# Pair weights requested before the last norm's squares, and a third block-product pair in the last MLP quarter

## The chip, the cores and the metric

One core of a Trainium2 chip runs the whole kernel. The metric is the device time of one execution in microseconds (us), the median of several runs. The engines are PE (TensorE, matrix products), ACT (ScalarE), DVE (VectorE), POOL (GpSimd) and SP (SyncE, which here issues DMAs). Each engine works through its own queue strictly in the order in which the program was built, and waits at an instruction until the results that it needs are there.

## The reference, cut to what matters

A decoder block on 512 tokens of 1024 channels: two attention mixers, then an MLP, then a last norm. The change touches the MLP's second product and the last norm alone:

```python
h = modulate(rmsnorm(x, g_mlp[layer]), sh_m, sc_m)
x = x + gt_m[:, None, :] * (jnp.square(jax.nn.relu(h @ w_fc1[layer])) @ w_fc2[layer])
...
return rmsnorm(x, g_final)
```

`w_fc1` is 1024 x 4096, `w_fc2` 4096 x 1024, everything float32.

## The kernel before, in words

Activations are kept transposed: a tile is 128 channels by 512 tokens, and `x` is eight such tiles (`xt`). A float32 operand is split into a high part (rounded to the PE's format by ACT) and a low part (the remainder, by DVE), and each product is three matmuls: high x high, high x low, low x high (`mm3`, L196).

The MLP runs in four quarters (`for qq in range(4)`). A quarter makes eight hidden tiles with `w_fc1` (24 matmuls of 512 columns each, `dense`), squares and splits them (`unit_relu` L913, `unit_parts` L918), and multiplies them with a quarter of `w_fc2`, adding the result to `xt`. The hidden tiles are made in the order `UNITS`; the first two of the next quarter are made ahead (`held`).

The second product goes by pairs of output tiles (`fc2_pair` L891). A pair is a 2 x 2 block matrix: two output tiles by two halves of the 1024 hidden channels of the quarter, times two halves of hidden channels by two halves of the tokens. With seven products of blocks in place of eight (sums of blocks taken beforehand) it needs 7 x 12 = 84 matmuls of 256 columns where plain products need 96. `pair_weights` (L826) prepares a pair: two DMAs of 512 KB (`raw[1]`, `raw[0]`), four sums of 128 x 512 on POOL (s1, s3, s2, s4 in that order: s2 is made from s1, s4 from s2), and the high and low parts of all blocks on ACT (L823) and DVE (L824). `pair_tiles` (L868) runs the products on PE in the order a11, s1, s3, s2, a12, s4, a22. Two accumulators are used twice: a12 adds into the bank of a11, and a22 into that of s3, so ACT first copies the bank out (L876 `u` after a11, L880 `e` after s3), and DVE adds s1's bank into `e` (L881) and s2's into `u` (L884) before s4 and the next pair use those banks. `sink` then adds the blocks into `xt` (DVE L898 to L905, and one sum `v` on POOL, L900).

In the last quarter only the first four output tiles go as pairs (`NH2 = 4` of the eight stay plain). I call those pairs A (tiles 0 and 1) and B (tiles 2 and 3). Tiles 4 to 7 are plain products by token halves: for each half 4 x 24 matmuls of 256 columns (L197 to L199), `mlp_out` (L808) with its square, then the norm of that half (`Stats.rstd` L149) and eight products into output tiles (L1018). So the first half's norm and output run under the second half's products. `Stats.add` (L128) takes a tile's square on ACT (L130) and adds it on DVE (L144); L911 and L813 scale the tile for the output on ACT.

What sets the order: nothing is ordered by hand here. The scheduler of the framework places instructions engine by engine when the program is built, by priority (the order of the code, with `tc.high_priority()` blocks first) and by its own estimate of what is ready. Buffers come from rotating pools: four for raw weights, three each for `w_hi` and `w_lo`, five of tag `p` (a pair's sums' high and low parts take four), three of tag `pT` (the four sums of a pair go through them), five of tag `tmp`. A buffer is written again only when its last reader is done.

Of the kernel before, what the change touches and what calls it, by code (L numbers as in the profile page):

```python
# [16 lines left out]
P = 128  # L17
S = 512
# [18 lines left out]
NH1 = 4  # L37
NH2 = 4
NPRE = 4
# [7 lines left out]
def block_kernel(ctx: ExitStack, tc: tile.TileContext, d):  # L47
# [777 lines left out]

    def pair_weights(src0, src1):  # L826

# [6 lines left out]
        for x_, y_ in ((a21, a22), (a11, a21), (0, a11), (2, a12)):  # L834
            t = sb.tile([P, S], F32, name="wsum", tag="pT", bufs=NB["pT"])
            nc.gpsimd.tensor_tensor(t, sums[x_] if isinstance(x_, int) else x_, y_, op=ALU.add)  # L836
            sums.append(t)
# [52 lines left out]

    def fc2_pair(qq, n):  # L891
        w = pair_weights(d["w_fc2"][qq, n], d["w_fc2"][qq, n + 1])

        def sink(pa, pb, pc, u, e):
            g0 = modb[:, GTM + n:GTM + n + 1]
            g1 = ngt[:, n + 1:n + 2]
            x0, x1 = xt[n], xt[n + 1]
            nc.vector.scalar_tensor_tensor(x0[:, T0], pa, g0, x0[:, T0], op0=ALU.mult, op1=ALU.add)  # L898
            v = tmp("v2")
            nc.gpsimd.tensor_tensor(v[:, T1], u, e, op=ALU.add)  # L900
            v1 = tmp("v1")[:, 0:HS]
            nc.vector.tensor_tensor(v1, u, pb, op=ALU.add)
            nc.vector.scalar_tensor_tensor(x0[:, T1], v1, g0, x0[:, T1], op0=ALU.mult, op1=ALU.add)
            nc.vector.tensor_tensor(v[:, T0], u, pc, op=ALU.add)
            nc.vector.scalar_tensor_tensor(x1, v, g1, x1, op0=ALU.mult, op1=ALU.add)  # L905

        pair_tiles(w, ub, sink)
        if qq == 3:
            for j in (n, n + 1):
                st2.add(xt[j])  # L910
                nc.scalar.activation(xt[j], xt[j], AF.Copy, scale=cols[:, C_GFIN + j:C_GFIN + j + 1])  # L911

    def unit_relu(pa, r):  # L913
# [48 lines left out]
    for qq in range(4):  # L962
# [11 lines left out]
        for i, n in enumerate(UNITS):  # L974
# [5 lines left out]
            else:  # L980
                w = wsplit(d["w_fc1"][8 * qq + n], (KT, P))
                pa = psum(("acc", "acc", "m", "o")[i % 4])
                dense(pa, w, h2)
            unit_parts(n, unit_relu(pa, tmp("relu")), ub, keep, qq == 3)

        held = {}
        if qq < 3:
            for i in range(2):
# [4 lines left out]
                held[i] = unit_relu(pa, r)  # L993
        nf = KT - NH2 if qq == 3 else KT
        for n in range(0, nf, 2):
            fc2_pair(qq, n)

    for k in range(4):
# [5 lines left out]
        ub.setdefault("12", []).append((hi, lo))  # L1004
    ws = [wsplit(d["w_fc2"][3, n], (KT, P), n < KT - 2) for n in range(nf, KT)]
    for hf, tok in enumerate(HALVES):
# [128 lines left out]
```

## Time and profile before

| | us |
|---|---|
| median of 3 runs | 817.91 |
| lowest and highest | 816.78 and 817.96 |
| the profiled execution's own time | 819.28 |
| its span in the profile | 817.5 |
| outside the span | 1.8 |

The profile is of one execution, which took 1.4 us longer than the median. Times below are us from the start of its span. The last quarter's second product starts at 759.31. A page line counts an engine as busy while any of its instructions runs. PE's instructions overlap, so a wait of PE shows as a jump between the starts of two neighbours: in the unstalled stretches they start about 0.12 us apart for 256 columns. A bracket behind a row gives the idle time before that instruction and what ended it.

### The profile page before, as it was taken

How to read it: one execution, taken by the hardware profiler on the slowest of the kernel's cores; microseconds unless marked ns; L12 is line 12 of the kernel's file. 1: busy time of each engine (PE TensorE's matmuls, PEld its weight loads, DVE VectorE, ACT ScalarE, POOL GpSimd, SP SyncE). 2: the span in 40 equal slices, each digit the busy share in tenths (PEclk: the TensorE clock that was granted, in tenths of full speed). 3: DMA queues.
4: the chain of work that ended last, by engine and by line, in shares of the span. 5: the costliest groups of instructions: out<-in, count | busy, mean ns of one | idle time of the engine just before them, and what ended most of it. 6: DMA issues, size and time to landing. Idle time of an engine off the chain costs nothing.

```text
span 817.5 us, 11881 instructions
## 1 busy us (share of the span) xinstructions
PE 795.0 (97%) x4444; PEld 645.4 (79%) x4444; DVE 605.3 (74%) x1186; ACT 385.7 (47%) x734; POOL 127.1 (16%) x116
## 2 busy tenths in 40 slices
PE   6999999999999999999999999999999999999896
PEld 3887668665577666888888998898899988998895
DVE  6989569878667778767676748886768676877854
ACT  4358437465324443323333446644564456445741
POOL 1000000001000000002200004450435043614200
PEclk9999999999999999999999999999999999999998
DMA  9972341010052034884357302333233422332303
GB/s 353 309 235 101 135 150 53 26 52 26 26 181 77 1 103 145 289 308 159 104 170 242 104 25 79 111 105 121 78 104 98 135 78 83 100 128 83 100 1 103
DMA packets 31004, 99.76 MB, mean 122 GB/s; under 512 B 3521, under 2 KB 5761, under 8 KB 30946
## 3 DMA queue, kind: packets, MB, share of 16 engines
q1 hardware_dynamic: 30880, 98.89, 36.3%
q8 instruction: 35, 0.57, 0.3%
q14 instruction: 23, 0.19, 0.1%
q0 software_dynamic: 64, 0.11, 0.0%
q10 hardware_dynamic: 2, 0.00, 0.0%
HBM read 96.89 MB, written 2.10 MB: 121 GB/s over the span
## 4 chain that ended last, share of the span: by engine, by line
PE 81%; DVE 5%; DMA 5%; ACT 4%; issue 3%; POOL 2%; SPq 0%; DVEq 0%; POOLq 0%; ACTq 0%
PE ps_acc L197 10%; PE ps_acc L199 10%; PE ps_acc L198 10%; PE ps_s L865 8%; PE ps_t L865 7%; PE ps_t L382 4%; PE ps_o L563 4%; DMA w_raw<-in_w_fc_dram 3%; PE ps_s L197 2%; PE ps_s L198 2%; PE ps_s L199 2%; PE ps_s L635 2%; PE ps_o L648 2%; POOL wsum L836 1%; PE ps_acc L258 1%
## 5 line engine op out<-in xcount | busy, mean ns | idle before, releaser
L183 ACT ACTIVATE w_hi<-w_raw 128x1024 fp32r<-128x1024 f32 x76 | 80.3, 1059 | 129.0 <-PE ps_acc L198 47.9
L184 DVE TENSOR_TENSOR w_lo<-w_raw,w_hi 128x1024 fp32r<-128x1024 f32 x76 | 99.4, 1309 | 51.4 <-ACT w_hi L183 51.1
L337 ACT ACTIVATE p<-p,nm 128x128 f32<-128x128 f32 (+3 forms) x96 | 53.3, 556 | 59.4 <-DVE nm L335 58.0
L199 PE MATMUL ps_acc<-hh,w_lo 128*128 128x512 f32 x200 | 80.2, 401 | 0.0
L198 PE MATMUL ps_acc<-hl,w_hi 128*128 128x512 f32 x200 | 79.7, 399 | 0.0
L197 PE MATMUL ps_acc<-hh,w_hi 128*128 128x512 f32 x200 | 79.6, 398 | 0.0
L370 DVE COPY pT<-ps_t 128x512 f32<-128x512 f32 (+1 forms) x72 | 42.3, 598 | 29.2 <-PE ps_o L563 16.4
L823 ACT ACTIVATE ws_hi<-wsum 128x512 fp32r<-128x512 f32 x56 | 35.3, 631 | 58.0 <-POOL wsum L836 55.4
L107 DVE SCALAR_TENSOR_TENSOR junk<-w_raw,cb 128x1024 bf16<-128x1024 f32 x32 | 38.5, 1220 | 19.0 <-DMA w_raw<-in_w_ada_dram 19.0
L836 POOL TENSOR_TENSOR wsum<-wsum,w_raw 128x512 f32<-128x512 f32 x28 | 45.6, 1630 | 25.8 <-DVE ws_lo L824 25.5
L836 POOL TENSOR_TENSOR wsum<-w_raw 128x512 f32<-128x512 f32 x28 | 39.2, 1400 | 65.2 <-DMA w_raw<-in_w_fc_dram 57.0
L824 DVE TENSOR_TENSOR ws_lo<-wsum,ws_hi 128x512 fp32r<-128x512 f32 x56 | 42.9, 797 | 4.9 <-PE ps_t L865 2.1
L198 PEld LDWEIGHTS ps_acc<-hl,w_hi 128*128 128x128 f32 x200 | 37.6, 188 | 10.9 <-issue 4.2
L197 PEld LDWEIGHTS ps_acc<-hh,w_hi 128*128 128x128 f32 x200 | 37.6, 188 | 10.8 <-issue 3.9
L199 PEld LDWEIGHTS ps_acc<-hh,w_lo 128*128 128x128 f32 x200 | 37.6, 188 | 10.4 <-issue 3.8
L197 PE MATMUL ps_acc<-h2h,w_hi 128*128 128x512 f32 x112 | 43.6, 389 | 0.0
L198 PE MATMUL ps_acc<-h2l,w_hi 128*128 128x512 f32 x112 | 43.6, 389 | 0.0
L199 PE MATMUL ps_acc<-h2h,w_lo 128*128 128x512 f32 x112 | 43.6, 389 | 0.0
L865 PE MATMUL ps_t<-t,ws_hi 128*128 128x256 f32 x224 | 40.5, 281 | 0.7 <-DVE t L953 0.4
L382 PEld LDWEIGHTS ps_t<-ident,p 128*128 128x128 f32 x240 | 27.6, 141 | 16.1 <-issue 5.4
L824 DVE TENSOR_TENSOR w_lo<-w_raw,w_hi 128x1024 fp32r<-128x1024 f32 (+1 forms) x28 | 31.1, 1110 | 10.2 <-ACT w_hi L823 10.2
L382 PE MATMUL ps_t<-ident,p 128*128 128x128 f32 x240 | 37.1, 279 | 0.0
(522 smaller groups left out, 2250.2 us busy)
## 6 DMA issues: line engine op xcount, KB each, us to landing
w_raw<-in_w_fc_dram SPq DMA_DIRECT2D x64, 512.0 KB, 3.3
w_raw<-in_w_ada_dram SPq DMA_DIRECT2D x32, 512.0 KB, 4.3
w_raw<-in_w_z_dram SPq DMA_DIRECT2D x25, 512.0 KB, 4.1
w_ada<-in_w_ada_dram SPq DMA_DIRECT2D x16, 512.0 KB, 5.7
w_raw<-in_w_c_dram SPq DMA_DIRECT2D x8, 512.0 KB, 4.8
w_raw<-in_w_o_dram SPq DMA_DIRECT2D x8, 512.0 KB, 4.8
w_raw<-in_w_out_dram SPq DMA_DIRECT2D x8, 512.0 KB, 3.3
w_raw<-in_w_g_dram SPq DMA_DIRECT2D x8, 448.0 KB, 6.6
```

Of the source, the lines that this page charges most:

```text
L107: nc.vector.scalar_tensor_tensor(junk, w, 1.0, cb, op0=ALU.mult, op1=ALU.mult, accum_out=mod[:, col:col + 1])
L183: nc.scalar.activation(hi[:, :n], raw[:, :n], AF.Copy)
L184: nc.vector.tensor_tensor(lo[:, :n], raw[:, :n], f(hi[:, :n]), op=ALU.subtract)
L197: nc.tensor.matmul(out, w[0], x[0], start=first, stop=False)
L198: nc.tensor.matmul(out, w[0], x[1], start=False, stop=False)
L199: nc.tensor.matmul(out, w[1], x[0], start=False, stop=last)
L337: nc.scalar.activation(o, o, AF.Exp, bias=nm, scale=-1.0, accum_out=sm)
L370: nc.vector.tensor_copy(dst, src)
L382: nc.tensor.transpose(pp[:, off:off + P], aps[i][:, kb * P:(kb + 1) * P], ident)
L824: nc.vector.tensor_tensor(lo, src, f(hi), op=ALU.subtract)
L836: nc.gpsimd.tensor_tensor(t, sums[x_] if isinstance(x_, int) else x_, y_, op=ALU.add)
L865: nc.tensor.matmul(out, w[a_][:, k], x[k][b_], start=(first and k == 0 and j == 0), stop=(k == 3 and j == 2), skip_group_check=True)
```

## The change

`pair_weights` is taken out of `fc2_pair`: the first pair's weights are asked for ahead of the loop, and each pair asks for the next pair's weights after its own products and before the squares of the last norm. `NH2` goes from 4 to 2, so in the last quarter tiles 4 and 5 become a third pair (C), and only tiles 6 and 7 stay plain, whose weights now lie in the `w_hi` and `w_lo` buffers. For pair B of the last quarter the first two sums (s1, s3) take `tmp` buffers (`wsum_t`) in place of `pT`. The parts of the last quarter's hidden tiles from the fifth on are made with high priority.

```diff
-NH2 = 4
+NH2 = 2
...
-    def pair_weights(src0, src1):
+    def pair_weights(src0, src1, late):
...
         for x_, y_ in ((a21, a22), (a11, a21), (0, a11), (2, a12)):
-            t = sb.tile([P, S], F32, name="wsum", tag="pT", bufs=NB["pT"])
+
+            if late and len(sums) < 2:
+                t = tmp("wsum_t")
+            else:
+                t = sb.tile([P, S], F32, name="wsum", tag="pT", bufs=NB["pT"])
...
-    def fc2_pair(qq, n):
-        w = pair_weights(d["w_fc2"][qq, n], d["w_fc2"][qq, n + 1])
+    def fc2_weights(qq, n):
+        return pair_weights(d["w_fc2"][qq, n], d["w_fc2"][qq, n + 1], qq == 3 and n == 2)
+
+    def fc2_pair(qq, n, w, more):
...
         pair_tiles(w, ub, sink)
+        ahead = fc2_weights(qq, n + 2) if more else None
         if qq == 3:
             for j in (n, n + 1):
                 st2.add(xt[j])
                 nc.scalar.activation(xt[j], xt[j], AF.Copy, scale=cols[:, C_GFIN + j:C_GFIN + j + 1])
+        return ahead
...
-            unit_parts(n, unit_relu(pa, tmp("relu")), ub, keep, qq == 3)
+            r = unit_relu(pa, tmp("relu"))
+            if qq == 3 and i > 3:
+
+                with tc.high_priority():
+                    unit_parts(n, r, ub, keep, True)
+            else:
+                unit_parts(n, r, ub, keep, qq == 3)
...
         nf = KT - NH2 if qq == 3 else KT
+        w = fc2_weights(qq, 0)
         for n in range(0, nf, 2):
-            fc2_pair(qq, n)
+            w = fc2_pair(qq, n, w, n + 2 < nf)
...
-    ws = [wsplit(d["w_fc2"][3, n], (KT, P), n < KT - 2) for n in range(nf, KT)]
+    ws = [wsplit(d["w_fc2"][3, n], (KT, P)) for n in range(nf, KT)]
```

The built order differs from the order before only in the last quarter, from its fifth hidden tile on; up to there, the first three quarters included, every engine's instructions stand as they stood. In the rows below `ws_hi` is the high part of a sum, `wsum` (or `wsum_t`) the sum, `w_hi` the high part of raw weights; the changed kernel's line numbers are shifted by the added lines (L823 is the same line in both, L915 before is L923, L939 is L947, L876 is L880, L836 is L840, L900 is L906).

Place 1, ACT while the last hidden tiles are made. Before (`wsum_7376` and `wsum_7378` are pair B's s1 and s3):

```order
L183 ACTIVATE w_hi_7186<-w_raw_7184 128x1024
L915 ACTIVATE relu_7085<-ps_acc_7060 128x512
L823 ACTIVATE ws_hi_7388<-wsum_7376 128x512
L928 ACTIVATE b12_6941<-relu_7085 128x256
L929 ACTIVATE ur2_7089<-relu_7085 128x256
L931 ACTIVATE uh2_7087<-ur2_7089 128x512
L823 ACTIVATE w_hi_7244<-w_raw_7232 128x1024
L915 ACTIVATE relu_7126<-ps_acc_7101 128x512
L823 ACTIVATE ws_hi_7388<-wsum_7378 128x512
L939 ACTIVATE relu_7126<-relu_7126 128x512
L940 ACTIVATE uh6_7128<-relu_7126 128x512
```

The same place on ACT in the changed kernel:

```order
L183 ACTIVATE w_hi_7186<-w_raw_7184 128x1024
L923 ACTIVATE relu_7085<-ps_acc_7060 128x512
L936 ACTIVATE b12_6941<-relu_7085 128x256
L937 ACTIVATE ur2_7089<-relu_7085 128x256
L939 ACTIVATE uh2_7087<-ur2_7089 128x512
L823 ACTIVATE w_hi_7244<-w_raw_7232 128x1024
L923 ACTIVATE relu_7126<-ps_acc_7101 128x512
L947 ACTIVATE relu_7126<-relu_7126 128x512
L948 ACTIVATE uh6_7128<-relu_7126 128x512
```

The two high parts of pair B's first sums have gone from between the hidden tiles' parts.

Place 2, POOL from the same time on to the end of its work. Before (`t3` is a part of a hidden tile, `v2_7358` and `v2_7498` the sums in pair A's and pair B's sinks, the four `wsum` are pair B's s1, s3, s2, s4):

```order
L948 TENSOR_TENSOR t3_7044<-relu_7037,b12_6941 128x256
L836 TENSOR_TENSOR wsum_7376<-w_raw_7373 128x512
L836 TENSOR_TENSOR wsum_7378<-w_raw_7372,w_raw_7373 128x512
L836 TENSOR_TENSOR wsum_7380<-wsum_7376,w_raw_7372 128x512
L948 TENSOR_TENSOR t3_7133<-relu_7126,b12_6941 128x256
L948 TENSOR_TENSOR t3_7222<-relu_7215,b12_6941 128x256
L836 TENSOR_TENSOR wsum_7382<-wsum_7380,w_raw_7372 128x512
L900 TENSOR_TENSOR v2_7358<-ue_7268 128x256
L900 TENSOR_TENSOR v2_7498<-ue_7408 128x256
```

The same place on POOL in the changed kernel (`wsum_t_7369` to `wsum_7375` are pair B's four sums, `wsum_7509` to `wsum_7515` pair C's):

```order
L956 TENSOR_TENSOR t3_7222<-relu_7215,b12_6941 128x256
L906 TENSOR_TENSOR v2_7358<-ue_7268 128x256
L840 TENSOR_TENSOR wsum_t_7369<-w_raw_7366 128x512
L840 TENSOR_TENSOR wsum_t_7371<-w_raw_7365,w_raw_7366 128x512
L840 TENSOR_TENSOR wsum_7373<-wsum_t_7369,w_raw_7365 128x512
L840 TENSOR_TENSOR wsum_7375<-wsum_7373,w_raw_7365 128x512
L840 TENSOR_TENSOR wsum_7509<-w_raw_7506 128x512
L840 TENSOR_TENSOR wsum_7511<-w_raw_7505,w_raw_7506 128x512
L840 TENSOR_TENSOR wsum_7513<-wsum_7509,w_raw_7505 128x512
L840 TENSOR_TENSOR wsum_7515<-wsum_7513,w_raw_7505 128x512
L906 TENSOR_TENSOR v2_7498<-ue_7408 128x256
```

Pair B's sums have moved from between the hidden tiles' parts to behind pair A's `v`, and pair C's four stand directly behind them.

Place 3, ACT in pair B of the last quarter. Before (`ue_7408` is pair B's `u` and `e`; `ps_s_7404` its a11 bank; `wp_hi` and `w_hi_7539` are weights of plain tiles):

```order
L823 ACTIVATE ws_hi_7394<-wsum_7380 128x512
L823 ACTIVATE ws_hi_7394<-wsum_7382 128x512
L823 ACTIVATE w_hi_7400<-w_raw_7373 128x512
L183 ACTIVATE wp_hi_7527<-w_raw_7525 128x1024
L183 ACTIVATE w_hi_7539<-w_raw_7537 128x1024
L130 ACTIVATE sq_7365<-xr0_3206 128x512
L911 ACTIVATE xr0_3206<-xr0_3206,cols_63 128x512
L130 ACTIVATE sq_7368<-xr1_3207 128x512
L876 ACTIVATE ue_7408<-ps_s_7404 128x256
L911 ACTIVATE xr1_3207<-xr1_3207,cols_63 128x512
L880 ACTIVATE ue_7408<-ps_t_7406 128x256
```

The same place on ACT in the changed kernel:

```order
L823 ACTIVATE ws_hi_7387<-wsum_7373 128x512
L823 ACTIVATE ws_hi_7387<-wsum_7375 128x512
L130 ACTIVATE sq_7397<-xr0_3206 128x512
L823 ACTIVATE ws_hi_7521<-wsum_7509 128x512
L918 ACTIVATE xr0_3206<-xr0_3206,cols_63 128x512
L823 ACTIVATE ws_hi_7521<-wsum_7511 128x512
L823 ACTIVATE ws_hi_7527<-wsum_7513 128x512
L130 ACTIVATE sq_7400<-xr1_3207 128x512
L880 ACTIVATE ue_7408<-ps_s_7404 128x256
L884 ACTIVATE ue_7408<-ps_t_7406 128x256
L823 ACTIVATE ws_hi_7527<-wsum_7515 128x512
```

Ahead of pair B's copy `u` (L880 in the changed kernel) now stand the high parts of pair C's s1, s3 and s2.

## Rows read from the trace of the kernel before

**Rows 1.** From the view of busy time by stretch: the two stretches around the start of pair A (columns: stretch, its length, then busy us and instruction count of PE, PE's weight loads, DVE, ACT and POOL, the granted clock as a share of 2.4 GHz, DMA share, GB/s).

```profile
760.00:770.00 10.00, 7.47 (x57) 6.67 (x56) 8.67 (x17) 7.45 (x17) 2.68 (x3) 1.00 0.17 53
770.00:780.00 10.00, 10.00 (x87) 10.00 (x86) 7.89 (x13) 6.99 (x12) 1.07 (x2) 1.00 0.34 107
```

**Rows 2.** From the view of waits, PE from 680 on (what waited, what it waited for, us in total, times, the longest).

```profile
PE ps_s L865 <- ACT uh L931: 1.5, 1, 1.5
...
PE ps_t L865 <- DVE t L953: 0.4, 1, 0.4
PE ps_s L865 <- DVE ul L932: 0.3, 1, 0.3
PE ps_t L865 <- ACT t L952: 0.3, 1, 0.3
```

**Rows 3.** From the timeline of PE (start, duration, instruction): the first matmul of pair A; the 35th of pair A (near the end of s3); pair A's first of a12; pair B's first of a12; the first plain matmul of the first token half, and the 49th.

```profile
759.31 0.28 PE L865 MATMUL ps_s<-uh,w_hi 128*128 128x256 f32 x1
...
766.72 0.39 PE L865 MATMUL ps_t<-t,ws_hi 128*128 128x256 f32 x1 [0.39 <-DVE t L953]
...
768.48 0.28 PE L865 MATMUL ps_s<-uh,w_hi 128*128 128x256 f32 x1
...
778.43 0.28 PE L865 MATMUL ps_s<-uh,w_hi 128*128 128x256 f32 x1
...
782.69 0.28 PE L197 MATMUL ps_s<-uh,wp_hi 128*128 128x256 f32 x1
...
788.35 0.28 PE L197 MATMUL ps_s<-uh,w_hi 128*128 128x256 f32 x1
```

**Rows 4.** From the timeline of ACT: the two high parts of pair B's first sums, the first part of a hidden tile behind the second of them, the last hidden tile's part that pair A's first product waits for, and pair A's copies `u` and `e`.

```profile
749.98 0.62 ACT L823 ACTIVATE ws_hi<-wsum 128x512 fp32r<-128x512 f32 x1
...
755.75 0.63 ACT L823 ACTIVATE ws_hi<-wsum 128x512 fp32r<-128x512 f32 x1 [1.98 <-POOL wsum L836]
756.29 0.62 ACT L939 ACTIVATE relu<-relu 128x512 f32<-128x512 f32 x1
...
761.37 0.62 ACT L931 ACTIVATE uh<-ur 128x512 fp32r<-128x512 f32 x1
...
764.96 0.37 ACT L876 ACTIVATE ue<-ps_s 128x256 f32<-128x256 f32 x1
...
767.26 0.38 ACT L880 ACTIVATE ue<-ps_t 128x256 f32<-128x256 f32 x1 [0.84 <-PE ps_t L865]
```

**Rows 5.** From the timeline of POOL: two sums of pair A while DVE was at work beside them, pair B's s3, pair B's s4, and pair A's `v`.

```profile
739.69 3.97 POOL L836 TENSOR_TENSOR wsum<-wsum,w_raw 128x512 f32<-128x512 f32 x2
...
754.43 1.28 POOL L836 TENSOR_TENSOR wsum<-w_raw 128x512 f32<-128x512 f32 x1 [7.33 <-DMA w_raw<-in_w_fc_dram]
...
768.30 1.33 POOL L836 TENSOR_TENSOR wsum<-wsum,w_raw 128x512 f32<-128x512 f32 x1 [2.85 <-DVE ws_lo L824]
769.59 0.74 POOL L900 TENSOR_TENSOR v<-ue 128x256 f32<-128x256 f32 x1
```

**Rows 6.** From the timeline of DVE: two low parts of sums and one low part of raw weights with POOL idle, two low parts of sums beside the first row of Rows 5, and the addition that ends pair A's `u`, beside pair B's s4 of Rows 5.

```profile
711.87 1.28 DVE L824 TENSOR_TENSOR ws_lo<-wsum,ws_hi 128x512 fp32r<-128x512 f32 x2
...
719.06 1.22 DVE L184 TENSOR_TENSOR w_lo<-w_raw,w_hi 128x1024 fp32r<-128x1024 f32 x1
...
740.73 3.47 DVE L824 TENSOR_TENSOR ws_lo<-wsum,ws_hi 128x512 fp32r<-128x512 f32 x2
...
768.73 0.41 DVE L884 TENSOR_TENSOR ue<-ue,ps_t 128x256 f32<-128x256 f32 x1
```

**Rows 7.** From the page's table of the costliest groups: the two groups of POOL's sums over the whole kernel (count | busy, mean ns of one | idle before, releaser).

```profile
L836 POOL TENSOR_TENSOR wsum<-wsum,w_raw 128x512 f32<-128x512 f32 x28 | 45.6, 1630 | 25.8 <-DVE ws_lo L824 25.5
L836 POOL TENSOR_TENSOR wsum<-w_raw 128x512 f32<-128x512 f32 x28 | 39.2, 1400 | 65.2 <-DMA w_raw<-in_w_fc_dram 57.0
```

**Rows 8.** From the timelines of DVE, ACT and PE at the end: the first half's eight outputs and the second half's first two tiles behind them; the last tile's addition; a square and the scaling behind it, and the last square; the last matmul of the first half and of the second.

```profile
798.31 2.74 DVE L1018 TENSOR_TENSOR out<-xr,ps_o 128x256 f32<-128x256 f32 x8 [0.62 <-PE ps_o L168]
800.96 1.01 DVE L809 SCALAR_TENSOR_TENSOR xr<-ps_s,modb,xr 128x256 f32<-128x256 f32 x2
...
807.53 0.48 DVE L809 SCALAR_TENSOR_TENSOR xr<-ps_s,modb,xr 128x256 f32<-128x256 f32 x1 [2.40 <-PE ps_s L199]
...
805.17 0.42 ACT L130 ACTIVATE sq<-xr 128x256 f32<-128x256 f32 x1 [1.89 <-DVE xr L809]
805.62 0.51 ACT L813 ACTIVATE xr<-xr,cols 128x256 f32<-128x256 f32 x1
808.05 0.42 ACT L130 ACTIVATE sq<-xr 128x256 f32<-128x256 f32 x1 [1.92 <-DVE xr L809]
...
793.99 0.28 PE L199 MATMUL ps_s<-uh,w_lo 128*128 128x256 f32 x1
...
807.21 0.28 PE L199 MATMUL ps_s<-uh,w_lo 128*128 128x256 f32 x1
```

**Rows 9.** From the view of busy time by stretch (columns as in Rows 1): two stretches after the last dense matmul.

```profile
809.00:810.00 1.00, 0.12 (x2) 0.04 (x1) 0.47 (x4) 0.27 (x2) 0.00 (x0) 0.86 0.00 0
810.00:811.00 1.00, 0.57 (x2) 0.29 (x2) 0.24 (x2) 0.00 (x0) 0.00 (x0) 0.50 0.00 0
```

**Rows 10.** From the timeline of PE: two transposes of 128 columns in the first half's norm, and two in the second's.

```profile
797.89 0.38 PE L168 MATMUL ps_o<-ident,rs_r 128*128 128x128 f32 x2
...
810.43 0.66 PE L168 MATMUL ps_o<-ident,rs_r 128*128 128x128 f32 x2 [1.30 <-DVE rs_r L165]
```

## The prediction

> **What bounds the kernel now.** I read the busy time by stretch first, then the waits of PE, then the timelines of the last 130 us, since the order changes only from the last quarter's fifth hidden tile on. PE bounds this end of the kernel. From 770 on it is busy all the time, and between 760 and 770 it is not: 7.47 of 10 us [rows 1]. Four waits make up those 2.5 us, all at the start of pair A and all for the last hidden tile's parts, from ACT and DVE [rows 2]. With no wait, 84 matmuls take 778.43 - 768.48 = 9.95 us, 0.1185 each [rows 3], and the plain tiles go at the same rate ((788.35 - 782.69) / 48 = 0.118). Pair A's 35th matmul starts at 766.72; unstalled it would be 759.31 + 34 x 0.1185 = 763.34. So the start of pair A loses 3.4 us (the waits and the restarts behind them), and nothing else before the last norm is lost. What follows in PE is 84 - 34 = 50 matmuls of A, 84 of B, 192 plain ones, then the second half's norm.
>
> **Part 1: the hidden tiles' parts no longer wait behind pair B's sums.** Before, ACT stands idle for 1.98 us at 753.77 for POOL's sum s3, makes its high part at 755.75, and only at 756.29 comes to the next hidden tile's part [rows 4]; POOL is at that sum since 754.43 [rows 5]. The changed order has neither the two high parts there nor the sums. That part can start at 753.8, 2.5 us earlier, and all that follows up to `uh` (761.37) is ACT's, DVE's and POOL's own chain, so it moves by the same; a further tenth or so comes from POOL being free for the hidden tile's `t3`. The next limit is near: the high part of pair B's raw weights, ahead of the last parts on ACT, needs the `w_hi` buffer that PE's last hidden tile holds until 759.3 [rows 3], about when ACT will be ready for it. I take 2.6: the 35th matmul starts at 764.1. Bounds: 3.4 (no wait left) and 1.5 (the longest wait alone). **-2.6.**
>
> **Part 2: pair C replaces two plain tiles.** 12 matmuls fewer on a PE without gaps: 12 x 0.1185 = **-1.4**. C's raw weights are no limit: their DMAs need only A's raw buffers, free once A's parts are made, before A starts, and POOL comes to them after 770.
>
> **Part 3: seven sums in a row on POOL, and `u` behind them on ACT.** This is a wait that the change adds. Before, B's first sums were made while the hidden tiles were still being made [rows 5], and only s4 was left. Now all four of B stand behind A's `v`, C's behind them, and ACT's copy `u` of B stands behind the high part of C's s2. PE's a12 of B adds into the bank that `u` empties, so PE waits for that copy.
>
> When would PE want it? From the 35th matmul at 764.1, 50 matmuls of A and 48 of B (a11, s1, s3, s2) are left: 764.1 + 98 x 0.1185 = 775.7.
>
> When can it have it? A's s2 product ends 14 matmuls after 764.1, at 765.8. DVE's addition into `u` takes 0.41 [rows 6] and starts some 0.2 behind its product, so `v` starts at 766.4 and ends, at 0.74 [rows 5], at 767.1. Then come seven sums: B's s1, s3, s2, s4, C's s1, s3, s2. A sum takes 1.28 undisturbed [rows 5], start to start a little less. But it isn't undisturbed: two sums took 3.97 while DVE made two low parts, and those took 3.47 instead of 1.28 [rows 5, 6]; 3.97 is 2 x 1.28 plus the two low parts' 1.28, so the two engines had taken turns, whole instruction by whole instruction. DVE's queue in this stretch is full of such work with two inputs in SBUF: seven low parts, one of 1.22, and two additions into `xt`. An addition with an input in PSUM (768.73) was not slowed beside a sum [rows 6]. I walk the two queues against each other in turns: six of the seven sums meet a low part or an addition and lose 0.2 to 0.5 each, 2.3 together. C's s3 loses 1.7 more, since it needs the `pT` buffer of B's s2, whose low part stands on DVE behind the 1.22 of C's raw weights and behind B's own s1 and s3. Together 7 x 1.28 + 2.3 + 1.7 = 13.0: C's s2 is there at 780.1. ACT's high part of it, a square of the same size and the copy `u` follow (0.53 + 0.53 + 0.38, stepping as in [rows 4]): 781.5. PE starts a12 5.8 us late. Part of that is already lost before it, in B's s1, s3 and s2, which wait for the same low parts; it is the same time and is not counted twice. The addition of s1's bank into `e` comes behind `u` on DVE, and s4 waits for it: 0.4. **+6.2.**
>
> Bounds: with no turns and no buffer wait 767.1 + 9.0 + 1.4 = 777.5, 1.8 late; with 1.98 for every sum (half of 3.97) and the buffer wait, 767.1 + 13.9 + 1.7 + 1.4 = 784.1, 8.4 and 0.4 late. The groups' means over the whole kernel, 1.40 for a fresh sum and 1.63 for one made from a sum [rows 7], give 4 x 1.40 + 3 x 1.63 = 10.5 and a12 at 779.0, 3.3 late. I take my walk, because those means are from stretches with half as many sums to a low part, while 3.97 is of the very mixture that stands here.
>
> The Trainium skill (SBUF — State Buffer, section Who interferes with whom) says that a DVE instruction with two SBUF inputs and a GpSimd instruction that reads SBUF exclude each other for the whole instruction. By that rule the sums come out as in my walk; by the means of the groups the change would come out 2.5 us faster than that.
>
> Behind `u` on ACT stands only what belongs to C and to the norm; C's products find their weights ready, since they start some 4 us after the last low part.
>
> **Part 4: the end.** The second half now has 2 tiles, 48 matmuls, under which the first half's norm and its eight outputs must pass. Before, the outputs end at 801.05, 6.8 us after the half's last matmul ended at 794.27 [rows 8]. The second half's PE work was 13.2 us (794.27 to 807.49), 11.4 for 96 matmuls and 1.8 for the norm's small ones and a bank wait; now it is 5.7 and some 1.6, and ends at 7.3. So both tiles' additions come right behind the outputs, and on ACT the last square waits for the first tile's square and scaling, 0.45 + 0.42 [rows 8]. From last matmul to end of last square it was 1.0 (807.49 to 808.47), now some 1.4: +0.4. In exchange no plain tile of the second half waits any more for a bank behind the outputs, as the third did before (two additions come at 800.96, behind them [rows 8]): -0.3. **+0.1.**
>
> **Sum:** -2.6 - 1.4 + 6.2 + 0.1 = +2.3. The profiled execution would go from 819.28 to 821.6. That one is 1.4 above the median of 817.91, and I put the same difference on the median: 820.2.
>
> **Rivals.**
> *Faster:* POOL and DVE hardly meet, so part 3 costs its lower bound, 1.8: -2.6 - 1.4 + 1.8 + 0.1 = -2.1, 815.8. For it: the sums at 754.43 and 768.30 ran at 1.28 and 1.33 [rows 5]. Against: DVE was idle or on PSUM inputs there. It decides from part 3 under 2.3 on.
> *No change:* the sums go at the groups' means [rows 7], part 3 costs 3.3 + 0.4 and gives back what parts 1 and 2 gain: -0.2, 817.7.
> *Slower still, by the clock:* PE's pause before a12 would be near 4 us, longer than any pause in [rows 2], through which the clock stayed at 1.00. After the last dense matmul, with PE almost idle, the granted clock fell from 1.00 to 0.50 between 809 and 810 [rows 9], from 2.4 to 1.2 GHz, and two transposes took 0.66 instead of 0.38 [rows 10], 1.7 times as long. If it falls in the new pause, each matmul behind it costs 0.08 to 0.12 more until it rises again; for 10 to 20 of them that is 1 to 2 us: 821.2 to 822.2. The Trainium skill (TensorE: Matmul & The Clock Gate, section HAM oscillation — how this bites in real kernels) says that pauses of PE between bursts of matmuls bring it down to the half clock; the stretch with the pauses of [rows 2] shows none of that, at 1.00 [rows 1].
> *The change doesn't do what it says:* for the first three quarters it certainly doesn't, their order is the same. In the last quarter part 1 could bring nothing, if the hidden tiles' parts are held by something else; then -1.4 + 6.2 + 0.1 = +4.9, 822.8. I see no such row.
>
> **How the numbers follow.** A difference of 0.2% is 1.6 us, about what a measurement of this kernel can tell from none. My forecast (819.5 to 822) has 0.48; the clock, a longer part 3 or no gain from part 1 (822 to 824) 0.20; no change 0.20; faster 0.12. Slower has 0.68 together. The likeliest is 820.2. Of the faster case all is left out, and of the upper one the half above 822.7: 816.9 to 822.7.
>
> **What would show it.** Part 1 is right if PE's waits for `uh` and `ul` at 760 to 763 are gone and A's 35th matmul starts near 764. Part 3 is right if PE waits for ACT's `u` copy before B's a12 (some 4 us) and for low parts before it, with POOL's seven sums filling 767 to 780 at over 1.6 each. Part 2 is right if pair C runs its 84 matmuls without a wait. I am wrong if PE reaches B's a12 by 779, which means that the sums passed DVE without turns, or if the order of ACT's queue costs nothing, because POOL is done with C's s2 by 776.

## The result and the profile after

The changed kernel took 822.92 us (median of four executions, 820.51 to 823.58) against 817.85 us for the kernel before (median of four, 816.78 to 817.96). The ratio is 1.0054, with a 95% interval of 1.0037 to 1.0071; the two medians alone would give 1.0062, which lies in that interval. The change makes the kernel slower, by 0.5%. Two later sets of executions gave 1.0042 (1.0027 to 1.0056) and 1.0041 (1.0028 to 1.0055). By the ratios the change costs 3.4 to 4.4 us, by the medians 3.6 to 5.1.

The profiled execution was the fastest of the four, 820.51 with a span of 818.7. Its first matmul of pair A starts at 757.55, 1.76 us earlier than before [rows 3], though the first instruction that left its place, pair B's s1 on POOL, stood only 14 us ahead of it (at 745.61 in the kernel before) and PE does not pause there. The two executions are 0.96 us apart already at 485 and 1.8 at 530, where nothing is changed. So I read both from that matmul on: 818.7 - 817.5 + 1.76 = 2.96 us is what the change costs in this pair of profiles.

From the view of waits of the changed kernel, PE from 740 on (as in [rows 2]):

```profile
PE ps_s L869 <- ACT ue L880: 3.4, 1, 3.4
...
PE ps_t L869 <- DVE ws_lo L824: 1.2, 1, 1.2
PE ps_s L869 <- DVE ws_lo L824: 0.4, 1, 0.4
PE ps_t L869 <- DVE t L961: 0.3, 1, 0.3
```

The four waits of [rows 2] for the last hidden tiles' parts have become one of 0.3. In their place stand two for low parts of pair B's sums and one of 3.4 us for the copy `u`. The timeline of PE in the changed kernel: the first and the 35th matmul of pair A, a wait in pair B's s2, the first two matmuls of pair B's a12, one 15 places behind the first of them, the first of pair C, and the last dense matmul.

```profile
757.55 0.28 PE L869 MATMUL ps_s<-uh,w_hi 128*128 128x256 f32 x1
...
762.08 0.39 PE L869 MATMUL ps_t<-t,ws_hi 128*128 128x256 f32 x1 [0.34 <-DVE t L961]
...
774.87 0.39 PE L869 MATMUL ps_t<-t,ws_lo 128*128 128x256 f32 x1 [1.19 <-DVE ws_lo L824]
...
779.74 0.58 PE L869 MATMUL ps_s<-uh,w_hi 128*128 128x256 f32 x1 [3.43 <-ACT ue L880]
780.12 0.41 PE L869 MATMUL ps_s<-ul,w_hi 128*128 128x256 f32 x1
...
783.07 0.28 PE L869 MATMUL ps_s<-uh,ws_hi 128*128 128x256 f32 x1
...
785.55 0.28 PE L869 MATMUL ps_s<-uh,w_hi 128*128 128x256 f32 x1
...
808.40 0.28 PE L199 MATMUL ps_s<-uh,w_lo 128*128 128x256 f32 x1
```

With [rows 3] and [rows 8] beside it the end falls into five stretches:

| stretch | before | after | difference | forecast |
|---|---|---|---|---|
| pair A, first to 35th matmul | 7.41 | 4.53 | -2.88 | -2.6 |
| to pair B's a12 (98 matmuls) | 11.71 | 17.66 | +5.95 | +5.8 |
| its a12, s4, a22 (36 matmuls) | 4.26 | 5.81 | +1.55 | +0.4 |
| to the last dense matmul | 24.52 | 22.85 | -1.67 | -1.4 - 0.3 |
| to the start of DVE's last eight outputs (811.12 and 812.34) | 3.91 | 3.94 | +0.03 | +0.4 |

The third line is the one that was forecast for another reason. Look at the durations there: the matmul at 780.12 shows 0.41 and its successors follow each other by 0.213; from 783.07 on it is 0.28, and 0.1185 as before. The busy time by stretch says why (columns as in [rows 1]):

```profile
770.00:780.00 10.00, 5.00 (x35) 4.40 (x36) 9.93 (x10) 5.16 (x10) 7.49 (x5) 0.98 0.23 85
780.00:790.00 10.00, 10.00 (x74) 10.00 (x75) 8.31 (x14) 5.68 (x9) 1.24 (x2) 0.85 0.00 0
```

PE is busy for half of the first stretch only, and the granted clock is 0.85 in the second, where it was 1.00 throughout before. Between 780 and 782 alone it is 0.50: behind the wait PE ran at 1.2 GHz, then at 2.4 again.

POOL in the changed kernel, from pair A's `v` to the sum s2 of pair C:

```profile
764.61 0.74 POOL L906 TENSOR_TENSOR v<-ue 128x256 f32<-128x256 f32 x1 [3.81 <-DVE ue L888]
765.31 2.99 POOL L840 TENSOR_TENSOR wsum_t<-w_raw 128x512 f32<-128x512 f32 x2
768.27 1.48 POOL L840 TENSOR_TENSOR wsum<-wsum_t,w_raw 128x512 f32<-128x512 f32 x1
769.82 1.61 POOL L840 TENSOR_TENSOR wsum<-wsum,w_raw 128x512 f32<-128x512 f32 x1
771.39 1.74 POOL L840 TENSOR_TENSOR wsum<-w_raw 128x512 f32<-128x512 f32 x1
774.95 1.61 POOL L840 TENSOR_TENSOR wsum<-w_raw 128x512 f32<-128x512 f32 x1 [1.82 <-issue]
776.53 1.71 POOL L840 TENSOR_TENSOR wsum<-wsum,w_raw 128x512 f32<-128x512 f32 x1
```

These are the seven sums: 11.1 us of work where 7 x 1.28 would be 9.0, and 1.82 of waiting at pair C's s3, from 765.31 to 778.24, 12.9 in all. The view names no releaser for that wait. C's s3 takes the buffer of B's s2, whose low part on DVE (the first of the two at 774.13) ends just before it. DVE beside the sums, where [rows 6] has 1.28 for two low parts of sums and 1.22 for one of raw weights:

```profile
768.51 3.46 DVE L824 TENSOR_TENSOR ws_lo<-wsum_t,ws_hi 128x512 fp32r<-128x512 f32 x2
...
772.23 1.98 DVE L824 TENSOR_TENSOR w_lo<-w_raw,w_hi 128x1024 fp32r<-128x1024 f32 x1
774.13 1.28 DVE L824 TENSOR_TENSOR ws_lo<-wsum,ws_hi 128x512 fp32r<-128x512 f32 x2
775.34 1.77 DVE L911 SCALAR_TENSOR_TENSOR xr<-v,ngt,xr 128x512 f32<-128x512 f32 x1
777.04 2.35 DVE L824 TENSOR_TENSOR ws_lo<-wsum,ws_hi 128x512 fp32r<-128x512 f32 x2
```

And ACT: the square of a hidden tile and the part of one that pair A's first product needs, which stood at 756.29 and 761.37 before [rows 4], and the queue ahead of `u`:

```profile
750.48 0.64 ACT L947 ACTIVATE relu<-relu 128x512 f32<-128x512 f32 x1
...
755.58 0.62 ACT L939 ACTIVATE uh<-ur 128x512 fp32r<-128x512 f32 x1
...
776.59 0.63 ACT L823 ACTIVATE ws_hi<-wsum 128x512 fp32r<-128x512 f32 x1 [2.19 <-POOL wsum L840]
778.26 0.63 ACT L823 ACTIVATE ws_hi<-wsum 128x512 fp32r<-128x512 f32 x1 [1.04 <-POOL wsum L840]
778.80 0.62 ACT L130 ACTIVATE sq<-xr 128x512 f32<-128x512 f32 x1
779.32 0.36 ACT L880 ACTIVATE ue<-ps_s 128x256 f32<-128x256 f32 x1
```

ACT stands idle for 2.19 and 1.04 us for pair C's sums, while pair B's a11 bank, which `u` copies, is complete since 769.7.

### The profile page after: what moved, and what is told of

Its sections match the earlier page's. It is cut to its first block, busy times and chain, and to the rows that moved or that the text cites. A ratio compares the mean times of both kernels' runs of the same rounds, so it can differ in the third digit from the quotient of the medians.

```text
span 818.7 us, 11874 instructions
## 1 busy us (share of the span) xinstructions
PE 795.4 (97%) x4432; PEld 645.6 (79%) x4432; DVE 614.7 (75%) x1191; ACT 388.1 (47%) x736; POOL 135.3 (17%) x121
## 4 chain that ended last, share of the span: by engine, by line
PE 84%; DVE 5%; ACT 4%; DMA 2%; issue 2%; POOL 1%; SPq 0%; DVEq 0%; POOLq 0%; ACTq 0%
PE ps_acc L199 12%; PE ps_acc L197 12%; PE ps_acc L198 11%; PE ps_s L869 8%; PE ps_t L869 6%; PE ps_t L382 4%; PE ps_o L563 4%; PE ps_s L635 2%; PE ps_s L197 2%; PE ps_s L198 2%; PE ps_s L199 2%; PE ps_o L648 2%; PE ps_acc L258 1%; PE ps_m L197 1%; PE ps_m L199 1%
## 5 line engine op out<-in xcount | busy, mean ns | idle before, releaser
L823 ACT ACTIVATE ws_hi<-wsum 128x512 fp32r<-128x512 f32 x58 | 36.6, 631 | 58.6 <-POOL wsum L840 55.9
L840 POOL TENSOR_TENSOR wsum<-wsum,w_raw 128x512 f32<-128x512 f32 x29 | 47.9, 1652 | 24.2 <-DVE ws_lo L824 23.8
L840 POOL TENSOR_TENSOR wsum<-w_raw 128x512 f32<-128x512 f32 x28 | 40.0, 1429 | 58.0 <-DMA w_raw<-in_w_fc_dram 47.9
L824 DVE TENSOR_TENSOR ws_lo<-wsum,ws_hi 128x512 fp32r<-128x512 f32 x58 | 45.2, 811 | 4.0 <-PE ps_t L869 2.6
L869 PE MATMUL ps_t<-t,ws_hi 128*128 128x256 f32 x240 | 43.3, 281 | 0.3 <-DVE t L961 0.3
L824 DVE TENSOR_TENSOR w_lo<-w_raw,w_hi 128x1024 fp32r<-128x1024 f32 (+1 forms) x30 | 34.1, 1137 | 11.2 <-ACT w_hi L823 11.1
L869 PE MATMUL ps_s<-uh,w_hi 128*128 128x256 f32 x120 | 34.7, 289 | 3.4 <-ACT ue L880 3.4
```

What stands on the lines that cost most here:

```text
L824: nc.vector.tensor_tensor(lo, src, f(hi), op=ALU.subtract)
L869: nc.tensor.matmul(out, w[a_][:, k], x[k][b_], start=(first and k == 0 and j == 0), stop=(k == 3 and j == 2), skip_group_check=True)
```

## The experiments

My theory after the result: pair B's first two sums, moved behind pair A's `v`, and pair C's after them hold POOL for 13 us, in turns with DVE; `u` waits behind them on ACT; and the pause that this makes in PE brings its clock down, which adds to it. The rivals: pair C costs by itself; the pace of the sums has a cause of POOL's own; the clock's loss is hidden. All medians, each beside the kernel before on the same chip (one chip for e1 to e4, one for e5 to e7, one for e8 to e10):

| kernel | median us | before us | ratio | 95% interval |
|---|---|---|---|---|
| e1, late sums undone | 816.77 | 817.72 | 0.9985 | 0.9974 to 0.9995 |
| e2, pause filled | 820.48 | 817.72 | 1.0038 | 1.0026 to 1.0050 |
| e3, two pairs | 819.05 | 817.72 | 1.0009 | 0.9998 to 1.0021 |
| e4, copies first | 817.69 | 817.72 | 1.0002 | 0.9993 to 1.0011 |
| e5, changed kernel again | 822.67 | 818.46 | 1.0042 | 1.0027 to 1.0056 |
| e6, sums on DVE | 814.64 | 818.46 | 0.9952 | 0.9939 to 0.9965 |
| e7, one input | 818.96 | 818.46 | 1.0010 | 0.9999 to 1.0021 |
| e8, PSUM input | 817.38 | 819.15 | 0.9983 | 0.9970 to 0.9995 |
| e9, pause filled, again | 821.10 | 819.15 | 1.0024 | 1.0014 to 1.0035 |
| e10, changed kernel, third | 822.76 | 819.15 | 1.0041 | 1.0028 to 1.0055 |

**e1: the late sums undone.**

```diff
     def fc2_weights(qq, n):
-        return pair_weights(d["w_fc2"][qq, n], d["w_fc2"][qq, n + 1], qq == 3 and n == 2)
+        return pair_weights(d["w_fc2"][qq, n], d["w_fc2"][qq, n + 1], False)
```

> The changed kernel with one thing undone: pair B's first two sums go into the buffers of all other sums again, not into two temporaries. In the order of its instructions POOL then makes B's s1, s3 and s2 between the hidden tiles, as before the change, and only s4 and pair C's sums are left behind pair A's v. Theory (the late sums are what costs: u on ACT stands behind seven sums): PE's waits at the start of pair A come back (3 to 3.5 us), B's a12 starts without a wait, pair C's 12 matmuls fewer stay. My walk of the queues gives 1.2 us less than before the change: 816.6, and 816 to 817.3. Rival (pair C itself costs, by its sums on POOL beside DVE's low parts, wherever B's are): slower than before, 819 to 821. Rival (asking ahead and the raised priority are what moves the hidden tiles' parts): pair A starts without the wait for the last hidden tile's parts, 813 to 815.

Measured: 816.77, 0.15% under the kernel before. Engine by engine, the order of this kernel is that of the kernel before with `NH2 = 2` and nothing else, instruction for instruction. So asking for the weights ahead of the squares and the raised priority move nothing by themselves; the buffers of two sums (`late`) are what moves POOL's order. With these buffers in place the raised priority still changes nothing in the built order, but asking ahead does: without it the changed kernel would have the same order on POOL, while ACT would have pair B's `u` ahead of the high parts of pair B's and C's sums. No run has that order, so how the cost divides between the buffers and the asking ahead is open. From the view of waits of this kernel, PE from 740 on:

```profile
PE ps_s L869 <- ACT uh L939: 1.2, 1, 1.2
PE ps_t L869 <- DVE t L961: 0.4, 1, 0.4
PE ps_s L869 <- DVE ul L940: 0.3, 1, 0.3
PE ps_t L869 <- ACT t L960: 0.3, 1, 0.3
```

The waits of [rows 2] are back at the start of pair A (7.12 us from its first to its 35th matmul), and there is none in pairs B and C. What is left is pair C's saving, as expected (816.6): both rivals fall.

**e2 and e9: the pause filled**, the same kernel in two sets of executions.

```diff
...
+        if fill:
+            junk = psum("o")
+            for _ in range(fill):
+                nc.tensor.matmul(junk[:, 0:HS], w["s2"][0][:, 3], b["t2"][3][0], start=True, stop=True)
         product(pa, w["a12"], b["21"], False)
...
-        pair_tiles(w, ub, sink)
+        pair_tiles(w, ub, sink, 24 if qq == 3 and n == 2 else 0)
```

> The changed kernel with 24 extra matmuls of 256 columns on PE between pair B's s2 and its a12 (into an unused bank; nothing reads them). They take 24 x 0.1185 = 2.84 us of a pause that was 3.43 us, so the work does not start later. Theory (in the changed kernel the granted clock falls in that pause, and in most executions stays down longer than in the profiled one): the clock stays at 1.00 there, the matmuls of a12 take 0.12 again and not 0.21, and the median falls from 822.9 to 819.2, that is below the profiled 820.5 by the 1.3 us of its 14 slow matmuls. Rival (the clock is not what parts the profiled execution from the others; the median's excess is noise of the start or of DMA): the median falls by 1.3 at most, 821.6 to 822.9. Rival (the pause is set by the work behind PE, and PE's own time does not count at all): 822.9 unchanged.

> The kernel with the filled pause once more, on the same chip as the changed kernel in the next run, since the two differ by little. Theory (behind the unfilled pause some 23 matmuls run at 0.21 and not 0.12, 2.2 us, against which the filled one has a new wait of 0.4 for B's s4): its median is 1.5 to 2.2 under that of the changed kernel, and its profile shows 1.00 throughout the end. Rival (the clock's loss is hidden by what follows): the two medians agree within 0.7.

Measured: 820.48, and 821.10 beside 822.76 for the changed kernel on the same chip, 1.7 us less although PE does more. That lies between my 819.2 and the rival's 821.6 in the first run, and inside the expectation in the second. Only the second set has both kernels side by side (818.82 to 822.37 for the filled one, 821.63 to 822.96 for the changed one); the first one's ratio of 1.0038 lies within the intervals of the changed kernel. Counted from pair A's first matmul to the end of the span, the profiles say the same: e2 and e9 take 2.2 and 2.1 us more than the kernel before, the changed kernel's three profiles 3.0, 3.9 and 4.5. The timeline of PE in e9, the extra matmuls and the start of a12, and the busy time by stretch:

```profile
777.93 3.00 PE L892 MATMUL ps_o<-t,ws_hi 128*128 128x256 f32 x24
781.55 0.39 PE L869 MATMUL ps_s<-uh,w_hi 128*128 128x256 f32 x1 [0.63 <-ACT ue L880]
781.78 0.28 PE L869 MATMUL ps_s<-ul,w_hi 128*128 128x256 f32 x1
```

```profile
780.00:790.00 10.00, 9.03 (x74) 8.63 (x74) 9.37 (x15) 6.86 (x13) 2.38 (x3) 1.00 0.01 2
```

The clock stays at 1.00 and the matmuls of a12 take 0.28. The wait for s4, which I had put into the sum at 0.4, appears here (0.36 in e2, 0.34 in e9), and the 36 matmuls from a12 on take 4.94 in e9; in the changed kernel the slow matmuls cover that wait.

**e3: two pairs, with the late sums.**

```diff
-NH2 = 2
+NH2 = 4
...
-    ws = [wsplit(d["w_fc2"][3, n], (KT, P)) for n in range(nf, KT)]
+    ws = [wsplit(d["w_fc2"][3, n], (KT, P), n < KT - 2) for n in range(nf, KT)]
```

> The changed kernel with two pairs in the last quarter and four plain tiles, as before the change: parts 1 and 3 without pair C. Theory: the start of pair A gains 2.9 as in the changed kernel (its 35th matmul comes 4.5 us after the first, not 7.4), but B's four sums still stand behind A's v; PE waits for low parts of B's s1 and s3 (0.3 to 0.5 each) and of s2 (0.3), and for the copy u some 2 us, since the square of pair A's second tile and two high parts of plain weights stand ahead of it on ACT. My walk gives 0.3 us more than before the change: 818.2, and 817.3 to 819. Rival (only C's sums hold u): no wait for u, and the gain of part 1 is kept: 815 to 816. Rival (part 1's gain was an accident of one profile): 820 or more.

Measured: 819.05, ratio 1.0009, 0.7 us over the kernel before by the ratio and 1.3 by the medians; the interval takes in 1. Pair A's 35th matmul comes 4.53 us after the first, as in the changed kernel; then, from the timeline of PE:

```profile
778.18 0.38 PE L869 MATMUL ps_s<-uh,w_hi 128*128 128x256 f32 x1 [1.74 <-ACT ue L880]
```

Even without pair C the late sums of pair B cost what they gain. The rival that only pair C's sums hold `u` falls, and so does the one that part 1's gain was an accident of one profile.

**e4: the copies first on ACT.** Pair C's high parts are queued behind pair B's copies, pair A's squares asked for behind pair B's tiles.

```diff
...
-        pair_tiles(w, ub, sink)
-        ahead = fc2_weights(qq, n + 2) if more else None
+        copied = pair_tiles(w, ub, sink)
+        with tc.issue_after(copied.ins) if qq == 3 and n in (2,) else ExitStack():
+            ahead = fc2_weights(qq, n + 2) if more else None
         if qq == 3:
-            for j in (n, n + 1):
+            for j in ((), (0, 1, 2, 3), (4, 5))[n // 2]:
```

> The changed kernel with ACT's queue reordered: pair C's high parts are queued behind pair B's copies u and e, and pair A's squares are asked for behind pair B's tiles. POOL's order of sums stays. Theory (u's place on ACT is the wait): u is made right behind B's a11, the 3.4 us wait of a12 is gone and with it the fall of the clock; what stays is the wait for B's s2 low part (1.2 to 1.4), and a new one of 1 to 2 us at the start of pair C, whose s1 low part comes later. My walk gives 0.3 less than before the change: 817.5, and 816.8 to 818.7. Rival (the sums' pace on POOL holds PE whatever the order on ACT): the wait moves whole to pair C, 821 or more.

(`copied` is pair B's copy `e`.) Measured: ratio 1.0002, 817.69. The timelines of ACT, pair B's copy `u`, of PE, pair C's s1, and of DVE just before that:

```profile
772.06 0.37 ACT L880 ACTIVATE ue<-ps_s 128x256 f32<-128x256 f32 x1
...
783.73 0.36 PE L869 MATMUL ps_s<-uh,ws_hi 128*128 128x256 f32 x1 [1.55 <-ACT sq L130]
...
781.97 1.28 DVE L824 TENSOR_TENSOR ws_lo<-wsum,ws_hi 128x512 fp32r<-128x512 f32 x2
783.17 0.41 DVE L909 TENSOR_TENSOR v<-ue,ps_s 128x256 f32<-128x256 f32 x1
```

`u` comes 7 us earlier than in the changed kernel, the wait of 3.4 and the fall of the clock are gone, and 1.3 at s2 and 1.55 at pair C's s1 are left. These two have the expected size, but not the expected cause. The low part of a block is first read by its third matmul, and here the first one waits. What it needs is its bank: DVE's addition at 783.17 reads pair B's s4 out of the bank that C's s1 writes, ends at 783.58, and stands on DVE behind two low parts. (The view names a square on ACT that ended at the same time; no product of pair C reads it.) B's s2 waits in the same way for an addition of pair A's. The order on ACT, the fall of the clock included, is worth 3.2 to 4.3 us (1.0002 against 1.0041 to 1.0054); the low parts on DVE then hold PE by way of the banks.

**e5 and e10: the changed kernel again**, unaltered, for more profiles.

> The changed kernel once more, unaltered, for more executions and a second profile: its first four executions took 820.5 (the profiled one) and 822.7 to 823.6. Theory (the pause before B's a12 brings the granted clock down, for longer in most executions than in the profiled one): the median is again 822 to 823, and this profile shows the clock under 1.00 for over 3 us behind that pause. Rival (the clock falls for some 3 us in every execution, and the first four were drawn high by what else varies): the median is 820.8 to 821.6, 1.3 to 0.4 over the kernel with the filled pause (820.5), and the profile shows the same 14 slow matmuls.

> The changed kernel, beside the kernel with the filled pause. Theory: 822 to 823, 4 to 5 over the kernel before, with 14 to 25 slow matmuls behind the pause in the profile. Rival: no more than 3 over the kernel before.

Measured: 822.67 and 822.76. The second is 3.6 us over the kernel before (3.4 by the ratio), under the 4 to 5 that I expected and over the rival's 3. From the timeline of PE in e5, pair B's a12, and from the busy time by stretch in e5 and in e10:

```profile
782.43 0.58 PE L869 MATMUL ps_s<-uh,w_hi 128*128 128x256 f32 x1 [3.43 <-ACT ue L880]
```

```profile
780.00:790.00 10.00, 7.57 (x45) 7.57 (x46) 7.78 (x13) 4.54 (x8) 3.24 (x3) 0.66 0.00 0
```

```profile
780.00:790.00 10.00, 9.32 (x55) 9.32 (x56) 7.36 (x13) 4.86 (x9) 2.19 (x2) 0.66 0.00 0
```

The wait is the same in all three profiles, 3.42 or 3.43. What differs is how long the clock stays down: the 36 matmuls from a12 on, 4.27 us at the full clock, take 5.81, 6.52 and 7.12. The matmuls that follow each other by 0.213 are 13, 21 and 27. Against 4.27 the clock costs 1.5, 2.3 and 2.9 us, the restart behind the wait included. But the slow matmuls also cover the wait for s4: against e9, where the same 36 take 4.94 at the full clock with that wait in them, they cost 0.9, 1.6 and 2.2. The first profile had the smallest loss of the three. One of the seven executions of e5 took only 819.02; there is no trace of it.

**e6: the sums of pairs B and C on DVE.**

```diff
...
-            nc.gpsimd.tensor_tensor(t, sums[x_] if isinstance(x_, int) else x_, y_, op=ALU.add)
+            eng = nc.vector if qq == 3 and n >= 2 else nc.gpsimd
+            eng.tensor_tensor(t, sums[x_] if isinstance(x_, int) else x_, y_, op=ALU.add)
...
```

> The changed kernel with the sums of pairs B and C (last quarter) made on DVE and not on POOL; buffers and places stay, the planner sets the order. Theory (seven sums of 1.3 on POOL, each in turns with DVE's low parts, are what holds u and the low parts): a sum costs DVE some 0.6, nothing takes turns with POOL, which has only v left; the start of pair A keeps its 2.9, PE's wait for u falls under 0.5, and no other wait is over 0.6. My walk gives 2.9 less than before the change: 815.0, and 814 to 816. Rival (DVE is already the fuller engine there, and eight more operations on it make it the bound): waits for low parts of over 1 us each at B's s1, s3, s2, and 818 to 821.

Measured: 814.64, 0.48% under the kernel before and 1% under the changed one on the same chip (e5): the best of all. The view of waits, PE from 740 on, has one row for `u`, and the timeline of DVE has the addition into `xt` (L912) and the addition of squares (L144) that took 1.77 and 1.61 beside POOL's sums:

```profile
PE ps_s L870 <- ACT ue L881: 0.4, 2, 0.3
```

```profile
773.44 0.75 DVE L912 SCALAR_TENSOR_TENSOR xr<-v,ngt,xr 128x512 f32<-128x512 f32 x1
...
775.43 0.69 DVE L144 TENSOR_TENSOR sq<-sq 128x512 f32<-128x512 f32 x1
```

A sum takes DVE 0.68 (POOL took 1.28 and more), and the rest of its queue is no longer held: DVE is busy for 9.9 of the 10 us from 770 to 780, as in the changed kernel, but with each operation at its own pace. The rival falls.

**e7: low parts with one input.** In pairs B and C the subtraction is left out; the low part is a multiple of the high part.

```diff
...
-            nc.vector.tensor_tensor(lo, src, f(hi), op=ALU.subtract)
+            if alone:
+                nc.vector.tensor_scalar(lo, f(hi), 1e-4, None, op0=ALU.mult)
+            else:
+                nc.vector.tensor_tensor(lo, src, f(hi), op=ALU.subtract)
...
```

> The changed kernel in which the low parts of pairs B and C are a multiple of the high part (an operation with one input in SBUF) and not the difference of two: the subtraction is left out. POOL's sums, their order and PE's work stay. Theory (POOL's sums and DVE's operations with two inputs in SBUF take turns): the sums beside the low parts take 1.28 to 1.33 again and not 1.5 to 1.75, only those beside A's additions into xt and its squares are longer; u comes some 4 us earlier, PE's wait for it is 1 to 1.5, and the time is 815 to 817. Rival (a sum takes 1.6 there for a reason of POOL's own, as its buffers or a sum as input): the sums stay at 1.5 to 1.75, the wait for u stays at 3 or more, and only the low parts themselves are shorter.

Measured: 818.96, over the theory's 815 to 817, and without the rival's wait of 3 us for `u`. The same operation on DVE with POOL idle and beside its sums, and two of the sums:

```profile
760.28 0.69 DVE L825 TENSOR_SCALAR w_lo<-w_hi 128x1024 fp32r<-128x1024 f32 x1 [1.49 <-ACT w_hi L823]
...
774.45 1.75 DVE L825 TENSOR_SCALAR w_lo<-w_hi 128x1024 fp32r<-128x1024 f32 x1
```

```profile
772.52 3.14 POOL L843 TENSOR_TENSOR wsum<-w_raw 128x512 f32<-128x512 f32 x2
```

This operation was held beside POOL too, so the run does not tell the theories apart. PE's wait moved from `u` to the low part of s2 (3.1 us).

**e8: low parts with one input in PSUM.** The subtraction is left out again; the low part is the high part times a bank of zeros.

```diff
...
+                for c in range(0, src.shape[-1], S):
+                    nc.vector.tensor_tensor(lo[:, c:c + S], f(hi)[:, c:c + S], zero, op=ALU.mult)
...
```

> The changed kernel in which the low parts of pairs B and C are the high part times a bank of zeros in PSUM, and not the difference of two operands in SBUF: the subtraction is left out, the operation keeps its size and reads one input in SBUF and one in PSUM. POOL's sums and their order stay. Theory (a sum on POOL takes turns with a DVE operation that uses both inputs from SBUF; the multiple of one input that was tried before takes its columns twice as fast, 0.69 for 1024, and was held beside POOL as well): the low parts take 0.7 beside POOL, the sums beside them 1.28 to 1.35, only those beside A's additions into xt and its squares are longer (1.5 to 1.8). PE's wait for u falls from 3.4 to 1.5 to 2.2, its wait for B's s2 goes, the clock stays at 1.00; time 815.5 to 817.5. Rival (POOL's sums take 1.5 to 1.7 whatever DVE reads there): the wait for u stays over 3, and the time over 819.

Measured: 817.38, ratio 0.9983. POOL and DVE in one stretch:

```profile
769.69 1.29 POOL L844 TENSOR_TENSOR wsum<-wsum,w_raw 128x512 f32<-128x512 f32 x1
770.94 3.00 POOL L844 TENSOR_TENSOR wsum<-w_raw 128x512 f32<-128x512 f32 x2
773.90 2.61 POOL L844 TENSOR_TENSOR wsum<-wsum,w_raw 128x512 f32<-128x512 f32 x2
```

```profile
770.08 1.45 DVE L919 SCALAR_TENSOR_TENSOR xr<-v,ngt,xr 128x512 f32<-128x512 f32 x1
771.45 1.27 DVE L828 TENSOR_TENSOR ws_lo<-ws_hi,ps_m 128x512 fp32r<-128x512 f32 x2
```

The low parts run at 0.63 each while POOL is at a sum. Of the eight sums, five take 1.27 to 1.31, one takes 1.48 and a pair 3.00. The one and the pair begin under additions into `xt` (the second of 1.45, 0.75 alone), and what they take over 1.28 each, 0.2 and 0.4, is no more than their overlap with these additions, 0.3 and 0.6; the low parts that run beside them for all the rest cost them nothing. The wait for `u` is 1.8, as in the prediction's bound with no turns and no buffer wait, and that for s2 is gone. So POOL's pace has no cause of its own: what DVE reads beside it sets it.

## Why the prediction was right, and where it was short

The direction was right, and so were the places of the terms and, but for the wait of s4 and the end, their sizes. The point, 820.2, is 2.7 under the median. The median lies 0.2 above the stated 816.9 to 822.7, and it falls among the cases from 822 to 824, to which the prediction gave 0.20, not into its forecast of 819.5 to 822. (By the ratio it would be 822.3, inside the range.) That is one step: the choice between the forecast and the rival with the clock.

*Part 1* (-2.6): -2.88. ACT comes to the hidden tile's square 4.0 us earlier (756.29 to 750.48, less the 1.76), not 2.5, but of the waits of 3.4 one of 0.3 is left, and PE can gain no more than that. It is left by the limit that the prediction names: ACT waits 1.02 us, to 757.52, for the buffer that PE's last hidden tile holds. What I had not seen is which edit does it: without the buffers the gain is gone (e1).

*Part 2* (-1.4) with the bank wait of part 4 (-0.3): -1.67 in one stretch.

*Part 3* (+5.8 up to a12): +5.95. The walk gave 13.0 for the seven sums, 12.9 was measured, with 1.82 for the buffer where I had 1.7. That POOL and DVE take turns is shown by e8, which leaves the sums on POOL and takes the second SBUF input from the low parts; that the sums on POOL are the price as a whole, by e6. The step from POOL to ACT is shown by e4. The Trainium skill (SBUF — State Buffer, section Who interferes with whom) says that a DVE operation with two SBUF inputs contends with a GpSimd instruction that reads SBUF, and so does one in a mode that uses the second port, which `tensor_scalar` can enter. The trace agrees with both: 1.77 for 0.75 in the first case, 1.75 for 0.69 in the second (e7), and 0.63 undisturbed with an input in PSUM (e8).

*The wait of s4* (+0.4) did not come in the changed kernel and did in the filled one (0.34): it is there only as long as the clock stays up.

*Part 4*, the end (+0.4): +0.03. The last square is 0.29 later where 0.4 was forecast (809.53 - 808.40 = 1.13 against 808.05 - 807.21 = 0.84), but the two transposes behind it took 0.40 and not 0.66 [rows 10]. The granted clock from 810 on was 0.73, and 0.50 before. Why it was higher is not settled; the prediction has no step for it.

*The clock* is where the forecast was short. I gave the rival 821.2 to 822.2, from 10 to 20 slow matmuls, and let it stand behind the forecast because the pauses of [rows 2] had passed at 1.00. They were of 0.3 to 1.5 us; the new one is of 3.4, with 1.2 just before it, and I had no row of a pause of that length under load but the end's [rows 9], where the clock did fall. In all three profiles it fell, and 13, 21 and 27 matmuls ran at half the pace. With s4's wait already in the forecast, the clock adds the 0.9, 1.6 and 2.2 us measured against e9, 1.5 in the mean. So the price that I gave the rival, 1 to 2 us, was of the right size; its place beside the forecast and not in it was wrong. The forecast of +2.3 becomes +3.8, and +3.4 to +5.1 was measured; without the fall of the clock, e2 and e9 show +2.0 to +3.1. The Trainium skill (TensorE: Matmul & The Clock Gate, section HAM oscillation — how this bites in real kernels) has it that such pauses between bursts bring PE to half the clock: here the trace agrees, with 0.50 between 780 and 782. The rule deserved to be part of the forecast, whose pause was longer than any in [rows 2].

## What to carry to other kernels

A tile's buffer pool is part of the order: two sums that were given other buffers ran 15 to 22 us later (e1 beside the changed kernel, from pair A's first matmul), and everything behind them on two engines moved with them. Where DVE takes two operands from SBUF beside a sum on POOL, count the work of both as one queue; the slower of the two engines is then no free help, and its work can be better off on the fuller one. A pause that a change puts into PE is to be priced with the slow matmuls that may come behind it.

## What the runs showed of the hardware

The same pause of 3.42 to 3.43 us was followed by 5.81, 6.52 and 7.12 us for the same 36 matmuls: the time at 1.2 GHz behind a pause differs between these three executions. They were not all on one chip, so what sets it is open. In e7 PE waited for 3.09 us in pair B's s2, and the granted clock stayed at 1.00:

```profile
770.00:780.00 10.00, 6.91 (x57) 6.63 (x56) 10.00 (x10) 6.77 (x13) 8.60 (x6) 1.00 0.33 107
```

That pause is 0.3 shorter, and no wait of 1.2 stands before it; what parts the two is not settled. And a kernel can gain by giving its fuller engine more to do: DVE makes a sum in 0.68 (e6), POOL in 1.28 at best [rows 5].
